# Two banks for the last half's roots, and v's second weights issued by ScalarE's queue

## The chip, the cores and the metric

The kernel runs on one core of one Trainium2 chip. The metric is the device time of one execution in microseconds. Before the change it is 700.87 us, the median of three runs (700.78 to 701.20).

A core has engines that run side by side, each through its own instructions in order: TensorE (PE in the profile, its loading of weights PEld), VectorE (DVE), ScalarE (ACT), GpSimd (POOL) and SyncE (SP), which only issues transfers. ScalarE and GpSimd can issue transfers as well; such an instruction stands in the engine's queue like any other, and what is behind it waits until it is issued.

## What is computed

One trunk layer on a sequence of 512 positions and 1024 channels, and a last RMS norm:

```python
h = rms_norm(x, norm_mix_g[l])
proj = h @ w_in[l]
cb, cc, cin, q, k, v, f_logit, g_logit = jnp.split(proj, split_idx, axis=-1)
u = causal_dwconv(cc * cin, conv_mix_w[l])
y_conv = (cb * u) @ w_out_conv[l]
o = forgetting_attention(q, k, v, log_f)      # heads of 64
y_attn = o @ w_out_attn[l]
x = x + (g_conv * y_conv + g_attn * y_attn) @ w_o[l]
h = rms_norm(x, norm_ffn_g[l])
up = causal_dwconv(h @ w_up[l], conv_ffn_w[l])
a, b = jnp.split(up, 2, axis=-1)
x = x + (jax.nn.silu(a) * b) @ w_down[l]
return rms_norm(x, norm_f_g)
```

`rms_norm` divides each position by the root of the mean of its squares (plus 1e-6) and scales each channel by a weight. Everything is float32.

## The kernel before

The activations lie transposed: 128 channels on the partitions, eight blocks of channels (kb = 0 to 7), 512 positions along the free dimension. Each float32 operand of a product is split into a high and a low part that TensorE can multiply in one pass each, and every product is three matmuls: high by high, weights' low by high, weights' high by low. For a weight tile, ScalarE (VectorE for the first two) makes the high part `wh`, VectorE the low part `wl`; for x, ScalarE makes `xgh` (line 468, with the norm's weight as a scale) and VectorE `xgl` (line 481).

**The start.** v comes first, since the rest of the attention needs it: eight blocks kb, each with weights `raw_v{kb}` (128 x 520) and a block of x, `xs{kb}` (128 x 512). TensorE works through them in order, 24 matmuls each, into six banks of PSUM: `pa0` to `pa3` (one per 128 positions) and `pb0`, `pb1`. Block kb = 0 is cut into halves of 256 positions: ScalarE converts the first half, then the second. In TensorE's order the four matmuls of the first half come first, then the four of the second half, each with the high parts, and so on. The transfers are issued in the order x0 (a first half of x with the norm's weights), v0 (its first 264 columns by ScalarE's queue, the rest by SyncE's), the second half of x's first block, then x1, v1, x2, v2 and so on, all by SyncE's queue (`load` and `load_x`). Before the first of these, seven matmuls on a tile of ones (`warm`, line 106) keep TensorE at work.

Eight semaphores (DMAHW0 to DMAHW7) are handed to the transfers of these queues in turn, in the order of the program. A transfer that gets a semaphore for the second time first waits until the earlier one on it has landed.

**The end.** The last blocks of channels (m = 6 and 7) of the down projection are summed in two halves of 256 positions, t = 0 and t = 1 (`plain7`). For each half `fin_sum` adds the residual, squares it (ScalarE, line 1210) and scales it; `fin_col` sums the squares over the channels by TensorE (`pc_n`, line 344) and takes the root (ScalarE) and its reciprocal (VectorE); `fin_out` spreads the reciprocal over all partitions by two matmuls into a bank of PSUM (`pb_n`, line 363), multiplies the eight blocks of channels by it, and issues their transfers out. VectorE multiplies blocks 0 to 5 in four products, reading the roots from PSUM (line 1226). [...]

## Time and profile before

| | us |
|---|---|
| median of three runs | 700.87 |
| the profiled execution | 700.85 |
| its span, first to last instruction | 699.1 |
| TensorE busy in the span | 688.4 |
| first matmul on v's weights, pa (start) | 4.08 |
| reciprocal of the second half (start) | 689.28 |
| GpSimd's last product (start, length) | 692.75, 1.26 |
| issue of the last transfer out (start) | 694.04 |

Times in the trace are counted from the span's start. A row of a timeline gives start, length, engine, line, operation, output and inputs, and in brackets how long the engine stood idle before and what ended it. "SPq" and "ACTq" are the issuing of transfers by SyncE and ScalarE. A row with x2 stands for two instructions in one piece. In a table by windows, each engine's busy time in the window is given with the number of its instructions, then the granted clock of TensorE, the share of the DMA engines' time that was busy, and the rate in GB/s.

### The profile page before, as it was taken

To read this page: it belongs to the slowest core of one execution; us is meant where nothing else is said; L and a number is where in the kernel's file an instruction comes from. 1 tells how busy PE (TensorE), PEld (TensorE's weight loads), DVE (VectorE), ACT (ScalarE), POOL (GpSimd) and SP (SyncE) were. 2 spreads that over 40 slices of the span, in tenths; PEclk is the share of its full clock that TensorE was granted. 3 is DMA by queue.
4 is the path that set the end of the run, shared out by engine and by line. 5 is a ranking of instruction groups with operands and counts; after the bars stand their busy time and mean duration, and the time that the engine had idled before them with its cause. 6 is when DMAs were issued, how large, how long until landed. Compare 5 with 4: busy or idle time off the path is not lost.

```text
span 699.1 us, 14571 instructions
## 1 busy us (share of the span) xinstructions
PE 688.4 (98%) x5978; PEld 686.1 (98%) x5978; DVE 506.6 (72%) x806; ACT 346.6 (50%) x551; POOL 159.6 (23%) x180
## 2 busy tenths in 40 slices
PE   9999999999999999999999999999999999999994
PEld 9999999999999999999999999999999999999994
DVE  6678777786687777764577877777775677877783
ACT  5574656555664443543445443455443345444662
POOL 5124646434011001035221212220000221200001
PEclk9999999999999999999999999999999999999998
DMA  8527877567359868758566647588675554334513
GB/s 313 184 85 204 206 153 186 132 167 177 96 143 272 254 179 241 233 183 206 144 156 175 168 111 214 144 182 224 192 225 178 147 147 99 102 99 139 161 60 121
DMA packets 54466, 118.91 MB, mean 170 GB/s; under 512 B 4960, under 2 KB 24416, under 8 KB 54400
## 3 DMA queue, kind: packets, MB, share of 16 engines
q1 hardware_dynamic: 39104, 96.55, 43.0%
q0 software_dynamic: 14576, 20.75, 18.6%
q8 instruction: 47, 0.77, 0.4%
q10 hardware_dynamic: 720, 0.69, 0.3%
q14 instruction: 19, 0.16, 0.1%
HBM read 115.80 MB, written 35.13 MB: 216 GB/s over the span
## 4 chain that ended last, share of the span: by engine, by line
PE 95%; DVE 2%; ACT 1%; issue 1%; ACTq 0%; POOLq 0%; POOL 0%; DVEq 0%
PE p_up L283 26%; PE p_in L283 14%; PE dn L301 13%; PE gs L301 8%; PE p_up L301 8%; PE p_wo L283 6%; PE yc L301 3%; PE ya L283 3%; PE pa L491 2%; PE pb L493 2%; PE p_g L283 2%; PE o L672 2%; PE tp L657 1%; PE pdA L283 1%; PE pdB L283 1%
## 5 line engine op out<-in xcount | busy, mean ns | idle before, releaser
L283 PE MATMUL p_up<-x1h,wh_up 128*128 128x256 f32 x536 | 104.8, 277 | 0.0
L283 PE MATMUL p_up<-x1l,wh_up 128*128 128x256 f32 x536 | 104.4, 276 | 0.0
L283 PE MATMUL p_up<-x1h,wl_up 128*128 128x256 f32 x536 | 104.3, 276 | 0.0
L250 ACT ACTIVATE wh_up<-raw_up 128x1024 fp32r<-128x1024 f32 x44 | 46.6, 1060 | 83.8 <-PE p_up L283 74.5
L139 POOL DMA_DIRECT2D sum<-in_wst_dram x51 | 52.7, 1108 | 125.3 <-DMA sum<-sum 89.1
L283 PEld LDWEIGHTS p_up<-x1h,wh_up 128*128 128x128 f32 x536 | 80.7, 188 | 0.5 <-issue 0.5
L283 PEld LDWEIGHTS p_up<-x1l,wh_up 128*128 128x128 f32 x536 | 80.8, 188 | 0.0
L283 PEld LDWEIGHTS p_up<-x1h,wl_up 128*128 128x128 f32 x536 | 80.6, 188 | 0.0
L254 DVE TENSOR_TENSOR wl_up<-raw_up,wh_up 128x1024 fp32r<-128x1024 f32 x44 | 54.1, 1230 | 16.1 <-ACT wh_up L250 16.1
L250 ACT ACTIVATE wh_F<-raw_F 128x1024 fp32r<-128x1024 f32 (+1 forms) x32 | 33.6, 1049 | 58.2 <-PE ya L283 25.9
L283 PE MATMUL p_in<-xgh,wh_in 128*128 128x256 f32 x288 | 56.8, 279 | 0.0
L283 PE MATMUL p_in<-xgh,wl_in 128*128 128x256 f32 x288 | 56.5, 277 | 0.1
L283 PE MATMUL p_in<-xgl,wh_in 128*128 128x256 f32 x288 | 56.4, 277 | 0.0
L989 DVE TENSOR_TENSOR fz<-p_up,rb_n 128x512 f32<-128x512 f32 x44 | 30.3, 690 | 32.4 <-PE p_up L283 32.4
L254 DVE TENSOR_TENSOR wl_F<-raw_F,wh_F 128x1024 fp32r<-128x1024 f32 (+1 forms) x32 | 38.6, 1207 | 20.0 <-ACT wh_F L250 19.3
L283 PEld LDWEIGHTS p_in<-xgh,wh_in 128*128 128x128 f32 x288 | 44.7, 188 | 0.7
L1002 POOL TENSOR_TENSOR ge<-fu,fu 128x512 f32<-128x512 f32 x11 | 17.1, 1552 | 120.2 <-DVE fu L586 107.2
L283 PEld LDWEIGHTS p_in<-xgh,wl_in 128*128 128x128 f32 x288 | 43.5, 188 | 0.3 <-DVE wl_in L254 0.3
L283 PEld LDWEIGHTS p_in<-xgl,wh_in 128*128 128x128 f32 x288 | 43.6, 188 | 0.0
L250 ACT ACTIVATE wh_P<-raw_P 128x768 fp32r<-128x768 f32 (+1 forms) x32 | 26.6, 832 | 27.3 <-PE dn L301 15.0
L301 PE MATMUL p_up<-x1h,wh_up 128*128 128x256 f32 x168 | 40.2, 276 | 0.0
L301 PE MATMUL p_up<-x1l,wh_up 128*128 128x256 f32 x168 | 40.2, 276 | 0.0
(319 smaller groups left out, 2033.1 us busy)
## 6 DMA issues: line engine op xcount, KB each, us to landing
raw_up<-in_wup_dram SPq DMA_DIRECT2D x44, 512.0 KB, 4.4
raw_F<-sum SPq DMA_DIRECT2D x31, 512.0 KB, 4.9
raw_in<-in_win_dram SPq DMA_DIRECT2D x24, 512.0 KB, 4.6
raw_P<-in_wst_dram SPq DMA_DIRECT2D x31, 384.0 KB, 3.6
sum<-in_wst_dram POOLq DMA_DIRECT2D x31, 256.0 KB, 5.7
sum<-in_wst_dram SPq DMA_DIRECT2D x15, 512.0 KB, 6.1
sum<-in_wst_dram POOLq DMA_DIRECT2D x15, 512.0 KB, 8.0
sum<-sum SPq DMA_DIRECT2D x30, 256.0 KB, 6.4
```

The costliest lines, as they stand in the source:

```text
L139: return lambda: keep(nc.gpsimd.dma_start(dst, src, accum_op=ALU.add))
L250: ins = nc.scalar.activation(hi, raw, AF.Copy)
L254: ins = nc.vector.tensor_sub(lo, raw, hi.bitcast(F32))
L283: keep(nc.tensor.matmul(out[:, cs], w, x[:, cs], start=start and i == 0 and c == 0, stop=stop and i == 2 and c == len(cut) - 1,))
L301: keep(nc.tensor.matmul(out, wl if x == 1 else wh, xl if x == 2 else xh, start=opens and bk not in seen, stop=closes and bk not in left,))
L491: keep(nc.tensor.matmul(pa[t][:, :VW], xt, w[:, :VW], start=start, stop=stop))
L493: keep(nc.tensor.matmul(pb[t], xt, w[:, VW:], start=start and t % 2 == 0, stop=stop and t % 2 == 1))
L657: keep(nc.tensor.transpose(tp[:, ks], pt[:, ks], ident))
L672: keep(nc.tensor.matmul(o[:, os_], vv[:, kb, pr, e, :], x[:, kb, cs], start=e == 0 and kb == 0 and i == 0, stop=e == 1 and kb == nk - 1 an ...
L989: nc.vector.tensor_mul(z, p, rb2)
L1002: keep(nc.gpsimd.tensor_mul(ge, a.rearrange(halves_of, h=2), b.rearrange(halves_of, h=2)))
```

## The change

There are two independent edits.

The first is at the start. `load` issues nothing for `raw_v1`; inside the conversion of x's block 0, ScalarE's queue issues that transfer, after the first half's conversion and before the second half's:

```diff
-            else:
+            elif k > 1:
                 keep(nc.sync.dma_start(raw[:, :ncol], src))
...
             for cs in cuts:
                 keep(nc.scalar.activation(xgh[:, kb, cs], x_of(kb, cs), AF.Copy, scale=g1(kb)))
+                if kb == 0 and cs.start == 0:
+                    keep(nc.scalar.dma_start(raws[1], stream[1][1]))
```

The second is in `fin_out`. In the first half (t = 0) the copy of the roots for GpSimd comes before VectorE's products instead of after them. In the second half the roots are made twice, in banks 4 and 2, one for VectorE and one for the copy. VectorE has three products of two blocks each instead of four, and the transfers out are four of two blocks each; in the second half ScalarE's queue issues the second and the last of them (GpSimd's).

```diff
-        pb = rstd_bc(rc, 2, (1, 4)[t], f"n3{t}")[:, : S // 2]
+        bks = ((1, 1), (4, 2))[t]
+        pb = rstd_bc(rc, 2, bks[0], f"n3{t}")[:, : S // 2]
+        pr = rstd_bc(rc, 2, bks[1], f"n3{t}r")[:, : S // 2] if t else pb
         rs = fp.tile([P, S], F32, tag="fu", name=f"rs{t}", bufs=3)[:, : S // 2]
-        parts_ = ((0, 1), (1, 3), (3, 5), (5, 6), (6, 8))
-        for a, b in parts_[:4]:
-            y = x1[:, a:b, hs]
-            keep(nc.vector.tensor_mul(y, y, pb.unsqueeze(1).to_broadcast([P, b - a, S // 2])))
-        keep(nc.scalar.activation(rs, pb, AF.Copy))
-        y = x1[:, 6:8, hs]
-        keep(nc.gpsimd.tensor_mul(y, y, rs.unsqueeze(1).to_broadcast([P, 2, S // 2])))
-        for g in (0, 1, 2, 3, 4):
-            a, b = parts_[g]
-            keep((nc.sync, nc.scalar)[t * (g in (1, 2))].dma_start(outT[:, a:b, hs], x1[:, a:b, hs]))
+
+        def by(e, r, g):
+            y = x1[:, 2 * g : 2 * g + 2, hs]
+            keep(e.tensor_mul(y, y, r.unsqueeze(1).to_broadcast([P, 2, S // 2])))
+
+        def copy():
+            keep(nc.scalar.activation(rs, pr, AF.Copy))
+
+        if t == 0:
+            copy()
+        for g in range(3):
+            by(nc.vector, pb, g)
+        if t:
+            copy()
+        by(nc.gpsimd, rs, 3)
+        for g in range(4):
+            keep((nc.sync, nc.scalar)[t * (g % 2)].dma_start(
+                outT[:, 2 * g : 2 * g + 2, hs], x1[:, 2 * g : 2 * g + 2, hs]
+            ))
```

How this moves instructions, at three places. First ScalarE at the start of the program, before (`xgh<-x` is the first half of block 0, `xgh<-xs,x` with 128x256 the second half, the one with 128x512 block kb = 1; in brackets the semaphores that each waits for):

```order
L204 DMA raw_v_132<-in_wv_dram 128x264
L468 ACTIVATE xgh<-x_130 128x256 [waits DMAHW0_49]
L468 ACTIVATE xgh<-xs_135,x_130 128x256 [waits DMAHW2_49]
L468 ACTIVATE xgh<-xs_135,x_130 128x512 [waits DMAHW3_49]
L455 ACTIVATE ssq_123<-x_130 128x256
```

and after:

```order
L204 DMA raw_v_132<-in_wv_dram 128x264
L468 ACTIVATE xgh<-x_130 128x256 [waits DMAHW0_49]
L470 DMA raw_v_138<-in_wv_dram 128x520 [waits DMAHW3_49]
L468 ACTIVATE xgh<-xs_135,x_130 128x256 [waits DMAHW2_49]
L468 ACTIVATE xgh<-xs_135,x_130 128x512
L455 ACTIVATE ssq_123<-x_130 128x256
```

The transfer stands ahead of the second half's conversion and waits for DMAHW3, the semaphore of x's block kb = 1; the conversion of that block needs no wait of its own any more.

TensorE's first matmuls on v, which are the same before and after but for their line numbers (here of the changed program; `pa_124` and `pa_125` take the first half of the positions, `pa_126` and `pa_127` the second):

```order
L493 MATMUL pa_124<-wh_v_151,xgh 128x264 [waits DVE_49,Activation_49]
L493 MATMUL pa_125<-wh_v_151,xgh 128x264
L495 MATMUL pb_128<-wh_v_151,xgh 128x256 [waits DVE_49]
L495 MATMUL pb_128<-wh_v_151,xgh 128x256
L493 MATMUL pa_126<-wh_v_151,xgh 128x264 [waits Activation_49]
L493 MATMUL pa_127<-wh_v_151,xgh 128x264
```

`pa_126` waits for ScalarE's second conversion, which now stands behind the transfer.

Then ScalarE at the end, before (`rs` is the copy of the roots, `sq_11` the square of the last block, `ms_n` the root):

```order
L350 ACTIVATE ms_n_8760<-pc_n_8755,ex 128x2 [waits PE_49]
L1227 ACTIVATE rs_8776<-pb_n_8773 128x256 [waits DVE_49,PE_49]
L1210 ACTIVATE sq_11_8800<-pdB_8636 128x256 [waits PE_49]
L1211 ACTIVATE x_4017<-pdB_8636,vec 128x256
L350 ACTIVATE ms_n_8812<-pc_n_8807,ex 128x2 [waits PE_49]
L1227 ACTIVATE rs_8825<-pb_n_8822 128x256 [waits DVE_49,PE_49]
L1232 DMA out_dram<-x_4017 128x2x256
L1232 DMA out_dram<-x_4017 128x2x256 [waits DMAHW6_49]
```

and after:

```order
L350 ACTIVATE ms_n_8760<-pc_n_8755,ex 128x2 [waits PE_49]
L1233 ACTIVATE rs_8776<-pb_n_8773 128x256 [waits PE_49]
L1212 ACTIVATE sq_11_8798<-pdB_8636 128x256 [waits DVE_49,PE_49]
L1213 ACTIVATE x_4017<-pdB_8636,vec 128x256
L350 ACTIVATE ms_n_8810<-pc_n_8805,ex 128x2 [waits PE_49]
L1233 ACTIVATE rs_8826<-pb_n31r 128x256 [waits PE_49]
L1243 DMA out_dram<-x_4017 128x2x256 [waits DVE_49]
L1243 DMA out_dram<-x_4017 128x2x256 [waits Pool_49]
```

Both copies wait for TensorE alone. The square's wait for VectorE is for the addition of the sums of squares before the reciprocal of the first half, not for the products. On VectorE the first half's products now wait for ScalarE's copy.

## The prediction

> **What bounds the kernel now.** I read the page first, then the chain of waits over the first 10 us, the timelines of the first and the last stretch, and the table by windows there.

> ```profile
> span 699.1 us, 14571 instructions
> ...
> PE 95%; DVE 2%; ACT 1%; issue 1%; ACTq 0%; POOLq 0%; POOL 0%; DVEq 0%
> ...
> PEld p_in L283 <- DVE wl_in L254: 0.3, 1, 0.3
> ```

> TensorE (PE) is 95% of the chain. The profiled execution took 700.85 us, 1.8 us more than its span and 0.02 us from the median, 700.87. So the sum can be made against 700.85. Nothing in the middle is edited: what counts is how early TensorE gets through its first blocks, and what is left after its last matmul. A delay at the start passes through whole, because between start and end the list of waits has nothing longer for TensorE than 0.3 us for a part of weights (its last row above; PEld is TensorE's loading of weights).

> The start, by the chain of waits (start, length, what):

> ```profile
> 1.05 3.35 PE warm L106 x14
> ...
> 5.39 0.56 PE pa L491 x2
> ...
> 6.82 0.42 PE pb L493 x2
> 7.25 0.25 PE pa L491 x2
> ...
> 8.45 0.23 PE pb L493 x2
> 8.68 0.30 PE pa L491
> ```

> From 1.05 on TensorE never stops. The first block of v (kb = 0) takes twelve pairs of matmuls, from 4.40 to 8.68. A pair takes about 0.43 until some 7.1, and 0.24 afterwards: the clock rises there, though the column of the granted clock reads 1.00 on both sides.

> ```profile
> 0.30:3.70 3.40, 2.65 (x12) 2.65 (x13) 0.23 (x2) 1.99 (x3) 2.92 (x13) 1.00 0.57 156
> 3.70:7.10 3.40, 3.40 (x17) 3.31 (x16) 2.30 (x5) 1.18 (x3) 3.22 (x7) 1.00 0.83 236
> ```

> In these windows (length, busy time of PE first) 2.65 us of work in 3.40 had not raised the clock; 3.40 of 3.40 had.

> **The start: what the change does.** ScalarE (ACT) and VectorE (DVE) there, by the timeline:

> ```profile
> 1.04 0.43 ACTq L204 DMA_DIRECT2D raw_v<-in_wv_dram  x1
> ...
> 3.64 0.91 DVE L248 CAST wh_v<-raw_v 128x264 fp32r<-128x264 f32 x2 [2.64 <-DMA raw_v<-in_wv_dram]
> ...
> 4.58 0.51 ACT L468 ACTIVATE xgh<-xs,x 128x256 fp32r<-128x256 f32 x1 [1.13 <-DMA xs<-in_xT_dram]
> ...
> 6.43 0.72 ACT L468 ACTIVATE xgh<-xs,x 128x512 fp32r<-128x512 f32 x1 [1.33 <-DMA xs<-in_xT_dram]
> ...
> 7.49 0.99 DVE L248 CAST wh_v<-raw_v 128x520 fp32r<-128x520 f32 x1 [1.42 <-DMA raw_v<-in_wv_dram]
> ```

> The transfer of v's second weights (raw_v1) goes from SyncE's queue to ScalarE's, between the two halves of the first conversion. The order shows that it waits there for DMAHW3, the semaphore on which the conversion of x's second block (kb = 1) waited before. So ScalarE stands until that block has landed. In the trace this is at 6.43. Queued behind are the second half of the first conversion (at 4.58 before) and all the rest of ScalarE. For that half waits TensorE's third pair (pa of positions 256 to 511), and TensorE works in order.

> Step by step: released at 6.43; the transfer's issue 0.43 (the row at 1.04), so 6.86; the half's conversion 0.51, so 7.37; some 0.05 to TensorE. It resumes at 7.42 where it went on at 5.39: a stall of 2.03 us with ten of the twelve pairs still to come. How long they take is set by the clock, which the trace does not show after a gap; I bound it:
> - Low: the clock is up at 7.1 as before. Ten pairs of 0.24 end at 9.82. But raw_v1 is then the last to come. The only such transfer by ScalarE's queue at the start went from 1.04 to 3.64, 2.6 us; from 6.43 this is 9.03, and with the 0.99 of the cast TensorE has its weights at 10.02, against 8.68 before. +1.3 us.
> - Middle: the clock needs another 3.4 us of unbroken work, as in 3.70:7.10, so until 10.8. By then 3.4 / 0.43 = 7.9 pairs are done, 2.1 follow at 0.24, end 11.3 against 8.68: +2.6 us. The cast at 10.02 is covered by TensorE's slow work.
> - High: it needs as long as the first time, 6.05 us from 1.05 to 7.1, so until 13.47. By then 14.1 pairs are done, which before stood at 8.68 + 4.1 x 0.24 = 9.66: +3.8 us.

> I take the middle, since the row nearest to it is the only full stretch that raised the clock; the first window, with 78% of work, did not, so a stretch with a stall of 2.03 us in it (3.70:7.10 would hold about half) should not either.

> [...]

> What the edit saves is nothing: SyncE's queue loses one issue of about half a microsecond, so x's third block and v's third weights come a little earlier, but TensorE needs those only one block of 2.9 us later than raw_v1. If raw_v1 came later than 11.3 instead of 9.03 it would cost its excess; 2.3 us cover that.

> **The end: what the change does.** Before (start, length; in brackets the idle time ahead and its releaser):

> ```profile
> 685.59 1.95 DVE L1226 TENSOR_TENSOR x<-x,pb_n 128x256 f32<-128x256 f32 x4 [1.16 <-PE pb_n L363]
> ...
> 686.68 0.28 PE L283 MATMUL pdB<-gl,wh_dp 128*128 128x256 f32 x1
> ...
> 687.64 0.38 ACT L1227 ACTIVATE rs<-pb_n 128x256 f32<-128x256 f32 x1 [3.40 <-DVE x L1226]
> ...
> 687.92 0.38 ACT L1210 ACTIVATE sq<-pdB 128x256 f32<-128x256 f32 x1
> ...
> 688.35 0.52 PEld L344 LDWEIGHTS pc_n<-ones,sq 128*128 128x128 f32 x4 [0.78 <-ACT sq L1210]
> ...
> 688.99 0.26 ACT L350 ACTIVATE ms_n<-pc_n,ex 128x2 f32<-128x2 f32 x1 [0.33 <-PE pc_n L344]
> ...
> 689.28 0.17 DVE L352 RECIPROCAL rc_n<-ms_n 128x2 f32<-128x2 f32 x1 [1.74 <-ACT ms_n L350]
> ...
> 689.61 0.61 PE L363 MATMUL pb_n<-ident,rc_n 128*128 128x128 f32 x4
> ...
> 690.25 1.95 DVE L1226 TENSOR_TENSOR x<-x,pb_n 128x256 f32<-128x256 f32 x4 [0.80 <-PE pb_n L363]
> ...
> 692.29 0.38 ACT L1227 ACTIVATE rs<-pb_n 128x256 f32<-128x256 f32 x1 [3.04 <-DVE x L1226]
> ...
> 692.75 1.26 POOL L1229 TENSOR_TENSOR x<-x,rs 128x512 f32<-128x512 f32 x1 [3.38 <-ACT rs L1227]
> ```

> *First half.* The copy of the roots (rs, 687.64) waited for VectorE's four products, and the square of the last product (687.92) queued behind it. Now the copy goes first (685.59), the products follow some 0.43 later and end at 687.9, and the square waits for nothing on VectorE that is late, only for TensorE's last matmul (686.68), through at about 687.0. TensorE's sum of squares then starts behind its own work ahead, which takes away the 0.78 idle. The reciprocal comes at 688.50, after the products with 0.6 to spare. -0.78 us for all that follows; between 0 and 0.78.

> *Second half.* Two more matmuls of the roots fill a second bank: four more entries, of which the row at 689.61 has four in 0.61, overlapping, so some 0.48 more. VectorE starts at 690.25 - 0.78 = 689.47. The second bank is full 0.45 to 0.5 later, at 689.95; copy 0.38, then 0.08, so GpSimd (POOL) starts at 690.45 beside VectorE and is through at 691.7, not at 694.01. The last transfer leaves when GpSimd is through; in the trace:

> ```profile
> 690.59 0.68 DVE L1226 TENSOR_TENSOR x<-x,pb_n 128x512 f32<-128x512 f32 x1
> ...
> 690.70 0.34 SPq L1232 DMA_DIRECT2D out_dram<-x  x1
> ...
> 694.04 0.38 SPq L1232 DMA_DIRECT2D out_dram<-x  x1
> ```

> So it goes at 691.75, 2.3 earlier. But four transfers of 256 KB must pass:

> ```profile
> 691.50:691.75 0.25, 0.00 (x0) 0.00 (x0) 0.25 (x1) 0.00 (x0) 0.00 (x0) 1.00 0.72 258
> 693.25:694.75 1.50, 0.00 (x0) 0.00 (x0) 0.00 (x0) 0.00 (x0) 0.77 (x1) 0.50 1.09 385
> ...
> 695.50:695.75 0.25, 0.00 (x0) 0.00 (x0) 0.00 (x0) 0.00 (x0) 0.00 (x0) 0.50 0.74 250
> 695.75:699.10 3.35, 0.00 (x0) 0.00 (x0) 0.00 (x0) 0.00 (x0) 0.00 (x0) 0.50 0.00 0
> ```

> (The last two columns are DMA share and GB/s.) Data flow 0.8 us after an issue (690.70 to 691.50), at 385 GB/s, so 262 KB take 0.69. VectorE's first two parts of eight are done at 689.47 + 0.68 = 690.15, data from 691.0; four transfers in a row end at 693.75, with small gaps 693.9, against 695.70. -1.8 us for the whole end. Bounds: -2.3 (the last issue alone) and -1.0 (nothing from the first half, since 0.78 falls away). What lies behind the last data, 3.35 us, stays.

> The nearest row with GpSimd working on as many elements while VectorE is busy is a product in the middle of the kernel:

> ```profile
> L1002 POOL TENSOR_TENSOR ge<-fu,fu 128x512 f32<-128x512 f32 x11 | 17.1, 1552 | 120.2 <-DVE fu L586 107.2
> ```

> It takes 1.55 there against 1.26 alone; 0.29 more would be half hidden by the transfers ahead. [...]

> **Sum.** 700.85 + 2.6 - 1.8 = 701.65; I say 701.6 us.

> **Rivals.**
> - *The clock stays low longer* (slower). The mechanism is the high bound, in TensorE after the stall: the clock takes as long to rise as at the start, and ten pairs and some of the next block go at half speed until 13.5. +3.8 - 1.8 = +2.0, 702.9. For it: 78% of work was not enough in 0.30:3.70. Against: after 7.42 there is no gap. [...] It decides above some 3.2 us at the start.
> - *The clock comes up on time*, or x's second block lands sooner with raw_v1 out of its queue: +1.3 - 1.8 = -0.5, 700.4. Against: half a window of work.
> - *No stall*: ScalarE is not held, and the change does what its words say, a transfer moved off a busy queue. Then the end alone counts, 699.0. The order speaks against it: the wait is on the instruction, ahead of the half that TensorE needs. It would take a landing before about 4.6, where the trace has 6.43.

> **How the numbers follow.** Forecast 0.60, late clock 0.20, early clock 0.14, no stall 0.06. Bounds together give -1.0 to +2.8; I leave out a little at each end: 700.2 to 703.2. A measurement here tells about 0.2%, 1.4 us, from no change. Faster by more needs no stall, 0.06. Slower by more: nearly all of the late clock and one part in eight of the forecast (a start of +2.9 with an end of -1.4), 0.27. Between: 0.67.

> **What would show it.** In the profile after: ScalarE's second half of xgh at about 6.9 instead of 4.58, TensorE idle some 2 us from 5.4, pairs of 0.43 after 7.4, the second block's matmuls at 11.3; at the end the square at 687.0 on before's scale, GpSimd beside VectorE, 3.35 us behind the last data. I am wrong if ScalarE's conversion stays at 4.6, if pairs of 0.24 follow the gap at once, or if the four last transfers leave gaps of 0.5.

## The result, and the profile after

The changed kernel takes 704.84 us (median of five runs, 702.78 to 706.49) against 700.94 for the kernel before (five runs beside them, 700.78 to 701.2): a ratio of 1.0055, with a 95% interval of 1.0037 to 1.0073. It is slower by about 3.9 us; the prediction was 701.6, in a range of 700.2 to 703.2. In these runs the changed kernel also scatters over 3.7 us where the one before stays within 0.4.

The profiled execution took 706.49 us, 1.77 more than its span, so it is read against before's 700.85. It is the slowest of the five, 1.65 above their median, so the losses read from it stand at the upper end. From the page:

```profile
span 704.7 us, 14570 instructions
...
PE 691.3 (98%) x5982; PEld 688.8 (98%) x5982; DVE 506.9 (72%) x804; ACT 346.6 (49%) x551; POOL 159.1 (23%) x180
...
PE 93%; DMA 2%; DVE 1%; ACT 1%; issue 1%; ACTq 0%; POOLq 0%; POOL 0%; SPq 0%; DVEq 0%
```

The chain of waits now contains DMA, 2% of it, which before's did not. Where, the chain over the first 20 us says (start, length, what):

```profile
2.12 5.75 DMA xs<-in_xT_dram
7.87 0.02 issue
7.89 6.74 DMA raw_v<-in_wv_dram
14.63 0.02 issue
14.65 0.44 DVE wh_v L248
15.10 0.14 issue
15.23 0.56 PE pa L493
...
18.17 0.22 PE pa L493
18.39 0.15 PE pb L495
18.54 0.12 PE pa L493
```

Two transfers in a row set the start. x's second block lands at 7.87; only then does ScalarE issue v's second weights, and they take 6.74 us. TensorE starts the second block of v at 15.23 where it started at 8.68 before, and at half the clock: matmuls of 0.22 until about 18.4, of 0.12 afterwards. Before's last matmul of the down projection stands at 686.68, here it is at 694.77 (below): the start costs 8.09 us in this execution.

TensorE's list of waits has the two stalls (total, times, longest):

```profile
PE pa L493 <- ACT xgh L468: 3.7, 1, 3.7
PE pa L493 <- DVE wh_v L248: 1.7, 1, 1.7
```

and the timeline who made them:

```profile
7.89 0.35 ACTq L470 DMA_DIRECT2D raw_v<-in_wv_dram  x1
...
8.29 1.12 ACT L468 ACTIVATE xgh<-xs,x 128x256 fp32r<-128x256 f32 x2 [4.84 <-DMA xs<-in_xT_dram]
...
8.85 0.81 PE L493 MATMUL pa<-wh_v,xgh 128*128 128x264 f32 x2 [3.73 <-ACT xgh L468]
...
14.65 0.43 DVE L248 CAST wh_v<-raw_v 128x520 fp32r<-128x520 f32 x1 [5.33 <-DMA raw_v<-in_wv_dram]
```

The first stall is ScalarE held in order at the transfer's wait, the second is the transfer itself. Of the 8.09 us, the two stalls are 5.4; the rest is half clock in the twelve pairs and beyond. The granted clock by windows (length, busy time of PE first; the column PEclk is the third from the right):

```profile
8.00:8.25 0.25, 0.00 (x0) 0.00 (x0) 0.00 (x0) 0.00 (x0) 0.25 (x2) 0.68 1.04 404
8.25:18.25 10.00, 7.72 (x34) 7.46 (x35) 4.05 (x7) 3.50 (x7) 1.66 (x3) 0.50 0.90 339
18.25:18.50 0.25, 0.25 (x4) 0.25 (x3) 0.11 (x1) 0.00 (x0) 0.00 (x0) 0.84 1.07 418
```

It fell at about 8.1, in the first stall, and was full again at 18.3.

The end, by the timeline of after (its scale is 8.09 us behind before's):

```profile
694.77 0.28 PE L283 MATMUL pdB<-gl,wh_dp 128*128 128x256 f32 x1
...
695.09 0.39 ACT L1212 ACTIVATE sq<-pdB 128x256 f32<-128x256 f32 x1 [1.02 <-PE pdB L283]
...
697.49 1.88 DVE L1230 TENSOR_TENSOR x<-x,pb_n 128x512 f32<-128x512 f32 x3 [0.80 <-PE pb_n L363]
697.93 0.38 ACT L1233 ACTIVATE rs<-pb_n31r 128x256 f32<-128x256 f32 x1 [1.45 <-PE pb_n31r L363]
698.40 1.27 POOL L1230 TENSOR_TENSOR x<-x,rs 128x512 f32<-128x512 f32 x1 [2.96 <-ACT rs L1233]
698.81 1.28 ACTq L1243 DMA_DIRECT2D out_dram<-x  x2
```

GpSimd multiplies blocks 6 and 7 by `rs`, the copy of the roots that ScalarE makes. The square no longer waits for VectorE's products of the first half, GpSimd works beside VectorE, and its product is as long there (1.27) as it was alone (1.26). The windows show the last data:

```profile
701.75:702.00 0.25, 0.00 (x0) 0.00 (x0) 0.00 (x0) 0.00 (x0) 0.00 (x0) 0.50 0.58 193
702.00:704.72 2.72, 0.00 (x0) 0.00 (x0) 0.00 (x0) 0.00 (x0) 0.00 (x0) 0.50 0.00 0
```

Data end about 7.2 us behind that last matmul (701.99 against 694.77), 9.1 before: 1.9 earlier. But behind the data only 2.73 us are left and no longer 3.3, so the end is shorter by 2.44: the span grew by 5.65, 8.09 less 2.44.

### The profile page after: what moved, and what is told of

The parts are those of the page before. It is cut to its first block, busy times and chain, and to the rows that moved or that the text cites. A ratio compares the mean times of both kernels' runs of the same rounds, so it can differ in the third digit from the quotient of the medians.

```text
span 704.7 us, 14570 instructions
## 1 busy us (share of the span) xinstructions
PE 691.3 (98%) x5982; PEld 688.8 (98%) x5982; DVE 506.9 (72%) x804; ACT 346.6 (49%) x551; POOL 159.1 (23%) x180
## 4 chain that ended last, share of the span: by engine, by line
PE 93%; DMA 2%; DVE 1%; ACT 1%; issue 1%; ACTq 0%; POOLq 0%; POOL 0%; SPq 0%; DVEq 0%
PE p_up L283 26%; PE p_in L283 14%; PE dn L301 13%; PE gs L301 8%; PE p_up L301 8%; PE p_wo L283 6%; PE yc L301 3%; PE ya L283 3%; PE pa L493 2%; PE p_g L283 2%; PE o L674 2%; PE pb L495 1%; PE tp L659 1%; PE pdA L283 1%; DMA raw_v<-in_wv_dram 1%
## 5 line engine op out<-in xcount | busy, mean ns | idle before, releaser
L283 PE MATMUL p_up<-x1h,wh_up 128*128 128x256 f32 x536 | 104.8, 277 | 0.0
L283 PE MATMUL p_up<-x1h,wl_up 128*128 128x256 f32 x536 | 104.4, 276 | 0.0
L283 PE MATMUL p_up<-x1l,wh_up 128*128 128x256 f32 x536 | 104.3, 276 | 0.0
L283 PEld LDWEIGHTS p_up<-x1h,wh_up 128*128 128x128 f32 x536 | 80.8, 188 | 0.5 <-issue 0.5
L283 PEld LDWEIGHTS p_up<-x1h,wl_up 128*128 128x128 f32 x536 | 80.7, 188 | 0.0
L283 PEld LDWEIGHTS p_up<-x1l,wh_up 128*128 128x128 f32 x536 | 80.6, 188 | 0.0
L254 DVE TENSOR_TENSOR wl_up<-raw_up,wh_up 128x1024 fp32r<-128x1024 f32 x44 | 54.1, 1230 | 16.8 <-ACT wh_up L250 16.8
L283 PE MATMUL p_in<-xgh,wh_in 128*128 128x256 f32 x288 | 56.8, 279 | 0.0
L283 PE MATMUL p_in<-xgh,wl_in 128*128 128x256 f32 x288 | 56.6, 278 | 0.1
L283 PE MATMUL p_in<-xgl,wh_in 128*128 128x256 f32 x288 | 56.5, 277 | 0.0
L254 DVE TENSOR_TENSOR wl_F<-raw_F,wh_F 128x1024 fp32r<-128x1024 f32 (+1 forms) x32 | 38.6, 1207 | 20.0 <-ACT wh_F L250 19.8
L283 PEld LDWEIGHTS p_in<-xgh,wh_in 128*128 128x128 f32 x288 | 44.7, 188 | 0.7
L1004 POOL TENSOR_TENSOR ge<-fu,fu 128x512 f32<-128x512 f32 x11 | 17.1, 1553 | 120.0 <-DVE fu L588 106.7
L283 PEld LDWEIGHTS p_in<-xgh,wl_in 128*128 128x128 f32 x288 | 43.6, 188 | 0.3 <-DVE wl_in L254 0.3
L283 PEld LDWEIGHTS p_in<-xgl,wh_in 128*128 128x128 f32 x288 | 43.6, 188 | 0.0
```

Of the source, the lines that this page charges most:

```text
L254: ins = nc.vector.tensor_sub(lo, raw, hi.bitcast(F32))
L283: keep(nc.tensor.matmul(out[:, cs], w, x[:, cs], start=start and i == 0 and c == 0, stop=stop and i == 2 and c == len(cut) - 1,))
L1004: keep(nc.gpsimd.tensor_mul(ge, a.rearrange(halves_of, h=2), b.rearrange(halves_of, h=2)))
```

## The experiments: the end

Two theories stood for the end. **D**: the data of the last transfers set it (the prediction). **G**: GpSimd sets it, with something that runs behind its last instruction. G came from the last pieces of the chain of waits, of before

```profile
689.38 3.34 issue
692.72 1.30 POOLq L1352
```

and of after:

```profile
694.14 1.29 POOL x L1230
695.43 2.93 issue
698.36 1.30 POOLq L1365
```

Both chains end in GpSimd's queue, neither in a transfer or in SyncE, which waits for the transfers. And in both the span ends 6.32 us behind the start of GpSimd's last product: 692.75 to 699.07, 698.40 to 704.72.

**e1_end_only**: the kernel before with the changed `fin_out` alone.

```diff
-        pb = rstd_bc(rc, 2, (1, 4)[t], f"n3{t}")[:, : S // 2]
+        bks = ((1, 1), (4, 2))[t]
+        pb = rstd_bc(rc, 2, bks[0], f"n3{t}")[:, : S // 2]
+        pr = rstd_bc(rc, 2, bks[1], f"n3{t}r")[:, : S // 2] if t else pb
...
+        if t == 0:
+            copy()
+        for g in range(3):
+            by(nc.vector, pb, g)
+        if t:
+            copy()
+        by(nc.gpsimd, rs, 3)
```

> The end as changed, the start as before. Theory G (the span ends 6.32 us after GpSimd's last product starts, as in the traces of before and of the change): that product starts 2.4 us earlier, so the time is 2.4 us lower, 698.5. Theory D (the span ends a fixed time after the last data, as the prediction had it): 1.8 to 1.9 lower, 699.0.

Measured: 698.5 us (698.35 to 700.12, seven runs) against 700.83, ratio 0.997 [0.9959, 0.998]. The end by itself is worth 2.3 us, as G says. Its chain of waits ends like the others, and 690.41 + 6.33 is its span, 696.74:

```profile
686.16 1.29 POOL x L1228
687.45 2.93 issue
690.38 1.30 POOLq L1363
```

**e11_first_half_only** and **e12_two_banks_only**: of the changed `fin_out`, one half of the positions each; the other half runs as before. Of e11 (e12 has `fin_old` for t = 0 in its place):

```diff
-    def fin_out(t, rc):
+    def fin_old(t, rc):
...
+    def fin_out(t, rc):
...
-    fin_out(1, rcB)
+    fin_old(1, rcB)
```

> The start as before; of the end only the first half as changed (the copy for GpSimd ahead of VectorE's products, three of them, four transfers), the second half as before. Theory G: the square no longer waits behind the copy, all of the second half comes 0.8 earlier, 700.1.

> The start as before; of the end only the second half as changed (two banks of roots, three products on VectorE beside GpSimd), the first half as before. Theory G: GpSimd's last product starts 0.9 behind VectorE's first and not 2.5, so 1.6 earlier, 699.3. Theory D (the transfers set the end): 1.1 lower at most, 699.8.

Measured: 700.01 us (ten runs, 699.95 to 700.26; 0.9987 [0.9978, 0.9996]) and 699.3 (ten runs, 699.18 to 699.35; 0.9975 [0.9966, 0.9984]), both beside a 700.94. That is -0.9 and -1.6, together -2.6; the two parts of `fin_out` add up to e1's -2.3 within the noise.

**e6_no_gpsimd_last**: e1, but in the last half VectorE makes the fourth product too. There is no copy, no second bank and no GpSimd behind the last matmul.

```diff
-        if t:
-            copy()
-        by(nc.gpsimd, rs, 3)
+        by(nc.vector if t else nc.gpsimd, pb if t else rs, 3)
```

> As e1, but in the last half VectorE makes the fourth product too, from the same bank, and GpSimd has nothing to do there. The last product ends 2.5 us after VectorE's start and not 2.2, so the last data come about as late as in e1 or 0.4 earlier. Theory G: GpSimd is through long before, the end is set by the transfers, 1.4 to 1.5 below e1, about 697. Theory D: 0 to 0.4 below e1.

Measured: 697.4 us (697.38 to 697.49, four runs), 0.9951 [0.9936, 0.9966]. Four products in a row on VectorE instead of three with GpSimd beside them, and the kernel is 1.1 us faster than e1. Its chain ends with VectorE's products:

```profile
689.44 0.69 DVE x L1229
690.13 0.60 DVEq L1362
690.73 1.20 DVE x L1229 x2
```

**e7_late_tiny_gpsimd**: e6, and one multiplication of a single column by GpSimd, which nothing reads, behind VectorE's last product.

```diff
+        if t:
+            fin_t = fp.tile([P, 1], F32, tag="fint", name="fin_t")
+            keep(nc.gpsimd.tensor_scalar(fin_t, x1[:, KB - 1, S - 1 : S], 1.0, 0.0, op0=ALU.mult, op1=ALU.add))
```

> As e6, with one product of a single column on GpSimd behind VectorE's last product, whose result nobody uses. No data goes out later. Theory G: the end moves to some 5 to 6.3 us behind this instruction, 1.9 to 3.1 above e6. Theory D: as e6 within 0.2.

Measured: 699.14 us (699.02 to 699.44, ten runs), 0.9976 [0.9966, 0.9986]: 1.74 more than e6, a little under what was expected. An instruction of 0.19 us that nobody waits for costs 1.7. The last data are at 693.9 in both kernels. Its row in the timeline:

```profile
692.09 0.19 POOL L1241 TENSOR_SCALAR fin_t<-x 128x1 f32<-128x1 f32 x1 [4.70 <-DVE x L1229]
```

What runs there stands in the raw trace, as an instruction DRAIN on GpSimd at the end of the program (us):

```
kernel   GpSimd's last work ends   its DRAIN          SyncE's waits end   span ends
before   694.02                    692.72 to 698.27   696.60              699.07
after    699.66                    698.36 to 703.93   702.88              704.72
e1       691.68                    690.38 to 695.94   694.89              696.74
e7       692.28                    692.05 to 696.54   694.83              697.3
e6       (none in the last half)   none so late       694.82              695.60
```

In the first four the DRAIN ends 4.3 us behind GpSimd's last instruction, 1.1 to 1.7 us later than all transfers are known to be through (SyncE's waits), and the span ends some 0.8 behind it. In e6 the end follows SyncE. So G holds: before and after the change GpSimd set the end, and the last data came second.

**e10_small_ends**: e6, with the last half's products and transfers cut into blocks of 1, 2, 2, 2 and 1, since now the data do count.

```diff
+        cuts = ((0, 1, 3, 5, 7, 8) if t else (0, 2, 4, 6, 8))
```

> As e6, with the last half's products cut into 1, 2, 2, 2 and 1 blocks and a transfer for each, so that data start to flow 0.24 earlier and the last transfer is half as long. In e6 nothing but the transfers is left to set the end (theory G), so 0.2 to 0.3 below e6, 697.15. If SyncE's and ScalarE's issuing is the limit there, it is as e6 or 0.1 above.

Measured: 697.25 us (697.1 to 697.31, four runs), 0.9947 [0.9934, 0.9961], 0.15 below e6, and 0.26 below it when each is taken against the kernel before that ran beside it. The two intervals overlap, so this last step is not clear of noise. It is the fastest median of all: the start as before, the first half as changed, no GpSimd in the last.

## The experiments: the start

Three things are in the edit: ScalarE is **held** until x's second block has landed; the transfer is issued **late**; and it stands in **another queue**. The theory after the result was that the late weights decide (L); the rivals were the hold, with its stall and its clock, and the queue.

**e2_head_only**: the first diff of the change alone, with the end as before.

> The start as changed, the end as before. Theory L (v's second weights, issued only after x's second block has landed, come in behind all that SyncE's queue had issued before): TensorE's second block of v starts at 14 to 15.5 us instead of 8.6, and the time is 4.3 to 8.1 us above before, by the clock, and scatters by some us. The prediction's theory (the stall between the two halves is the cost): 2.6 us above, 703.5.

Measured: 708.53 us (706.81 to 709.72, four runs), 1.0107 [1.0093, 1.0121]: +7.6. Its profile, of the slowest of the four (709.72), has ScalarE released at 8.19, the cast of v's second weights at 15.35, and stalls of TensorE of 3.3 and 2.6 us. +7.6 here and -2.3 in e1 make +5.3, where the median of the change is +3.9. That is inside the scatter of after (+1.8 to +5.6), so the two edits can be independent; closer than this the runs do not show it.

**e4_hold_only**: the transfer stays in SyncE's queue as before; ScalarE is held in the same place by converting x's second block there.

```diff
             for cs in cuts:
                 keep(nc.scalar.activation(xgh[:, kb, cs], x_of(kb, cs), AF.Copy, scale=g1(kb)))
+                if kb == 0 and cs.start == 0:
+                    keep(nc.scalar.activation(xgh[:, 1, :], x_of(1, slice(0, S)), AF.Copy, scale=g1(1)))
...
-        if kb == 1:
-            x_hi()
```

> As before, v's second weights by SyncE's queue in their old place; but ScalarE converts x's second block between the two halves of the first, so that it stands until that block has landed, as in the change. Only the hold is left. The prediction's theory: TensorE stalls from 5.4 to about 7.7 and the time is 2.6 to 3.8 us above before. Theory L: the hold is the smaller part of the change's cost, some 2.3 to 4 alone, and below e2 by 2 us or more.

Measured: 704.77 us (704.27 to 705.84, five runs), 1.0057 [1.0044, 1.0069]: +3.85. TensorE has one stall, and v's second weights are in time:

```profile
PE pa L491 <- ACT xgh L468: 2.9, 1, 2.9
```

The clock came up at 13.31. The hold with everything it does to the clock therefore costs about what the high bound of the prediction said (+3.8), and no more. That the two agree so well is partly luck: the stall was 2.9 us and not the 2.03 of the prediction.

**e5_late_no_hold**: the transfer is issued behind both halves of the first conversion, so that it holds nothing that the first block needs.

```diff
-                if kb == 0 and cs.start == 0:
+                if kb == 0 and cs.start > 0:
                     keep(nc.scalar.dma_start(raws[1], stream[1][1]))
```

> As e2, but the transfer stands behind both halves of the first conversion, ahead of the conversion of x's second block. ScalarE holds up nothing that TensorE needs early; only the weights are late. Theory L: TensorE runs on until 8.7, then idles until 14 to 15.5; time as e2 within 1 us. The prediction's theory: nothing is lost but what the weights come later than 8.6 by a price of 2.6 us from 6.4, that is 702.3 at most.

Measured: 709.53 us (707.1 to 710.32, four runs), 1.0127 [1.0111, 1.0142]: +8.6, no less than the whole edit at the start (e2, +7.6). There is no hold; its list of waits and its chain, of the fastest of the four, at 707.1:

```profile
PE pa L493 <- DVE wh_v L248: 4.9, 1, 4.9
```

```profile
2.11 5.30 DMA xs<-in_xT_dram
...
7.43 5.19 DMA raw_v<-in_wv_dram
...
12.65 0.44 DVE wh_v L248
```

So the late transfer is enough for the loss, and the hold is not needed for it. The two are no sum: with both, TensorE waits for the same late weights and the hold fills part of that time.

**e8_other_semaphore** was to give the transfer another semaphore to wait for, by a tiny transfer (one column, read by nobody) behind the loading loop.

```diff
+    shift = ap.tile([P, 1], F32, tag="shift", name="shift")
+    keep(nc.sync.dma_start(shift, vecs[:, :1]))
```

> As e2, with one tiny transfer (one column) on SyncE's queue ahead, so that the transfer of v's second weights gets another semaphore, that of v's first weights, which have landed by 3.6. Everything else of the start stands as in the change. Theory L in its full form (the wait for x's second block makes the issue late, the queue does the rest): issued at about 3.5, in about its old place, so the second block starts within 1 us of before; 700.9 to 701.9. If issuing by ScalarE's queue is itself the cost: 703 or more.

A miss: the tiny transfer came too late in the order, and the wait was the same as in e2. Measured 706.64 us (705.62 to 707.17, five runs), 1.0079 [1.0066, 1.0091]; issue at 7.48, cast at 12.53. It is in effect a second e2. In its execution (705.62, the fastest of the five) TensorE stalls for 3.1 us on ScalarE and not at all on the weights: its slow first block still covered them. So with the hold, the weights add to the loss only where they come later than that.

**e9_free_semaphore**: the same tiny transfer inside the loop, between the loads of x's second block and of v's second weights. The transfer by ScalarE now stands where the change puts it, but it waits for the transfer of v's first weights. That one landed at 3.46, when ScalarE's first conversion (to 3.44) was just through, so the wait holds nothing.

```diff
     for kb in range(1, AHEAD + 1):
         load_x(kb)
+        if kb == 1:
+            keep(nc.sync.dma_start(shift, vecs[:, :1]))
         load(kb)
```

> The start as changed, the end as before, and a tiny transfer (one column) on SyncE's queue between x's second and third block, so that the transfer of v's second weights, in the change's place between the two halves on ScalarE, now waits for the transfer of v's first weights instead of x's second block (e8 had put the tiny transfer too late, and its wait was still that of the change). Theory L (the wait for x's second block is the cause, by the hold and by the place in line that is lost): issued at about 3.6, landed by 8, TensorE's second block within 1 us of before, 700.9 to 701.9. If the place on ScalarE's queue is the cost: as e2 and e8, 705 or more.

Measured: 702.68 us (702.57 to 704.12, six runs), 1.0028 [1.0017, 1.004]: +1.75 where e2 has +7.6. Most of the loss hangs on which semaphore the transfer was given, that is on a wait for a transfer with which it has nothing to do. It did not go away altogether (700.9 to 701.9 was expected). The wait and the chain:

```profile
PE pa L496 <- DVE wh_v L248: 1.6, 1, 1.6
```

```profile
3.48 5.82 DMA raw_v<-in_wv_dram
...
9.32 0.44 DVE wh_v L248
```

The transfer left at 3.48, 0.9 us later than SyncE had issued it before (2.60), and still took 5.8 us; TensorE waits 1.6 us for it.

**e3_at_once**: the transfer directly behind that of v's first weights in ScalarE's queue, without any wait.

```diff
-                keep(nc.sync.dma_start(raw[:, :ncol], src))
+                keep((nc.sync, nc.scalar)[k == 1].dma_start(raw[:, :ncol], src))
```

> The end as before; v's second weights by ScalarE's queue, but issued directly behind the transfer of v's first weights, ahead of every conversion, with a semaphore that no earlier transfer has. If the wait ahead of the issue is what costs, this costs nothing: 700.9 within 0.6. If ScalarE's queue is slow for such a transfer once SyncE's queue is full, the second block of v starts some us late and the time is 703 or more.

Measured: 701.1 us (700.82 to 704.0, ten runs), 1.0007 [0.9998, 1.0017]: no difference. Issued at 1.51, when little is under way, the weights landed at 5.38, in 3.9 us. In this run ScalarE's queue by itself was no disadvantage, and it brought nothing either. In this execution TensorE waits for the second half of x's first block, converted at 5.58; with the start as before that stood between 4.14 and 5.42, so it is not shown that the early weights pushed it back.

```profile
PE pa L491 <- ACT xgh L468: 1.1, 1, 1.1
```

**e14_late_long_queue** and **e13_late_short_queue** (one execution each) ask why a late transfer is so slow. In e14 it is issued behind the conversion of x's second block, at 7.58. e13 is the same, but the program starts with two blocks loaded ahead and not four, so that fewer transfers were issued before; later blocks then come late as well, and only the transfer is compared, not the time.

```diff
-AHEAD = 4
+AHEAD = 2
```

> The start as in e5 (the end as before), but the transfer of v's second weights stands behind the conversion of x's second block and waits for no semaphore of its own: issued as late as in the change, at 6.5 to 7.5 us, with SyncE's queue as full as there. Whatever makes the transfer slow: 5 to 7 us from issue to cast, as in e5 (5.2) and the change (6.7).

> As e14, but only two blocks are loaded ahead and not four (three buffers for weights), so SyncE's queue holds fewer transfers when that of v's second weights is issued, at 6.5 to 7.5 us. If the transfers issued earlier are what it waits behind: 3 to 4.2 us from issue to cast, at least 1 us less than e14. If a transfer by ScalarE's queue takes long whatever is ahead: as e14 within 0.5. Its whole time says nothing, since the rest of the kernel loads less far ahead too.

Measured: 707.79 us and 710.81 us, beside 700.91. The transfer in the two chains, of e14:

```profile
7.58 5.75 DMA raw_v<-in_wv_dram
```

and of e13:

```profile
7.34 3.95 DMA raw_v<-in_wv_dram
```

With ten transfers issued ahead of it, as in e13, it takes 1.8 us less than with twelve, as in e14. In e14 its first data move at 10.44, 2.9 us after the issue, and in e13 at 8.79, after 1.45. One pair of executions is thin evidence, since the executions with twelve ahead differ among themselves by more than this (5.1 to 7.2 from issue to cast, below).

The traces hold a better one. A transfer of this size lands in sixteen shares, and the time of each is recorded. In all sixteen traces, the transfers that SyncE and ScalarE issued in the first 10 us begin to land in the order of their issue, whichever of the two issued them. Before, the first six were issued at 0.73, 1.04 (by ScalarE), 1.18, 1.65, 2.12 and 2.60 and began to land at 2.66, 3.15, 3.49, 3.86, 4.85 and 6.01. So a transfer has a place in one order of issue. In the changed kernel the weights are the 13th in it: what SyncE issued just before them, at 6.12, begins to land at 10.88, the weights at 11.54, what SyncE issued next at 13.49. Before, they were the 6th. In order of the place, with the issue, the end of the landing, VectorE's cast and the time from issue to cast (us):

```
kernel   place   issue   landed   cast    issue to cast
e3         4     1.51     5.38     6.53   5.0   (VectorE is late, not the weights)
before     6     2.60     7.47     7.49   4.9   SyncE's queue
e9         8     3.48     9.29     9.32   5.8   the tiny transfer ahead
e13       11     7.34    11.29    11.31   4.0   two blocks ahead
e8        13     7.48    12.50    12.53   5.1   the tiny transfer ahead
e5        13     7.43    12.63    12.65   5.2
e14       13     7.58    13.32    13.35   5.8
after     13     7.89    14.63    14.65   6.8
e2        13     8.19    15.32    15.35   7.2
```

The further back the place, the later the landing; and in the kernel before, the transfers in the 4th, 8th, 11th and 13th place landed at 4.56, 9.07, 11.09 and 12.43, all of SyncE's queue (the 4th only half a block of x). So the change moved the weights from the 6th place to the 13th, and in these traces their lateness goes with this loss of place. No run issues them late by SyncE's queue; that it would bring little is an estimate, from SyncE's transfer in the 13th place before, 5.6 us from issue to landing (6.79 to 12.43). Why the five executions with the 13th place lie 2.8 us apart is open.

## Why the prediction was wrong

**Right.** That ScalarE is held by the wait for x's second block, that TensorE's third pair stands behind it, that the clock is lost by this, and that a delay at the start goes through whole (7.99 us at TensorE's first sum of squares, 34.69 against 26.70, and 8.09 at the last matmul of the down projection). At the end: the reordering of the first half, -0.78 predicted and -0.9 measured alone (e11), with the square at 695.09, which is 687.0 on before's scale; the data, 1.8 us earlier predicted and 1.9 measured; GpSimd beside VectorE without a loss.

The last one was put into the sum without a row: no row of the kernel before shows that GpSimd beside VectorE takes no longer than its 1.26 us alone, and the nearest row, a product in the middle of the kernel, had 1.55. In the changed kernel the product took 1.27 us, 0.97 of them beside VectorE's products (697.49 to 699.37), which had one operand in PSUM (`pb_n`).

**The step that failed** is the price of the late transfer: "The only such transfer by ScalarE's queue at the start went from 1.04 to 3.64, 2.6 us; from 6.43 this is 9.03", and, resting on it, "The cast at 10.02 is covered by TensorE's slow work". The row at 1.04 was of an issue with one transfer ahead of it (SyncE's at 0.73), and of 264 columns where the second weights have 520. At 7.89 the transfer had twelve issued ahead of it and took 6.74 us. The cast came at 14.65, far beyond the 11.3 that the prediction named as the end of its cover. TensorE was through with its slow first block at 13.55, waited 1.7 us, and then went on at half clock to 18.3. A nearer row was there: the same weights by SyncE's queue, issued at 2.60 and cast at 7.49, 4.9 us with five transfers issued ahead. By it the cast would begin at 6.43 + 4.9 = 11.33 and the weights be there at 12.3, 1.0 beyond the cover of 11.3; the same sum would have said 702.7, slower. Nearer still is the place in the order of issue: the 13th transfer of the kernel before, issued at 6.79, landed at 12.43. With the cast that is 13.4, 2.1 beyond the cover, and the sum would have said 703.8.

**Mis-sized beside it.** x's second block released ScalarE at 7.89, not at 6.43. The value was that of one execution; in the fifteen other executions it lies between 6.44 and 8.19 (6.48 to 7.29 in the six whose start is that of before), and 6.43 is the earliest. It is not scatter alone. In the six kernels whose SyncE queue goes straight from x's second block to its third (after, e2, e5, e8, e13, e14) it lies between 7.33 and 8.19, in the ten others between 6.43 and 7.29. So taking the weights out of their place goes with a later landing of x's second block, the opposite of what the rival of the early clock allowed for; why is not shown. This alone is 1.5 us.

**The clock** did not go by the middle assumption (3.4 us of unbroken work from 7.42). With the weights in time, the hold alone cost +3.85 (e4) where this term had +2.6. The trace records from when to when the full clock was granted (us):

```
before  7.11 to 693.19
after   4.68 to 8.09, 18.33 to 701.00
e1      5.56 to 695.05
e2      5.91 to 9.33, 12.74 to 16.15, 19.57 to 702.23
e3      4.25 to 693.74
e4      13.31 to 695.98
e5      6.46 to 13.29, 16.70 to 699.37
```

**The end.** "What lies behind the last data, 3.35 us, stays" was wrong, and with a small effect. What lies there is no fixed tail behind the transfers but GpSimd's DRAIN, 4.3 us behind its last instruction. GpSimd's last product starts 2.44 us earlier against the last matmul (6.07 before, 3.63 after), and that is the gain, not the 1.9 of the data. The prediction had the lower bound of -2.3 for "the last issue alone" and put it aside for the data; that this number is near is luck, since it was reckoned for the last transfer and not for GpSimd. The chain of waits of before, read to its last row, already ended in POOLq.

**The sum.** 700.85 + 2.6 - 1.8 = 701.65 was predicted; 700.85 + 8.09 - 2.44 = 706.50 is the profiled execution, 706.49. The 4.85 us between them are 5.49 that the start cost more than predicted, less 0.64 that the end saved more. Of the 5.49, 1.70 is the first stall (3.73 for 2.03), 1.68 the second, and the remaining 2.1 the half clock beyond what was reckoned.

**What stays open.** How the loss at the start divides between hold, lateness and clock cannot be given as a sum, since they overlap: alone they cost +3.85 (e4) and +8.6 (e5), together +7.6 (e2). Why the changed kernel scatters from 702.8 to 706.5 was not followed run by run; the varying grid of the clock and the varying arrival of x's second block and of the weights could each do it. Nor was it tried whether another order of SyncE's early transfers would make e9 as fast as before.

## What to carry to other kernels

A transfer that is moved into an engine's own queue takes its semaphore's wait with it, and the engine can stand in order behind a transfer that has nothing to do with it (here ScalarE stood until 7.89 us; the start cost 7.6 us in e2 and 1.75 in e9, where the transfer waited for one that had landed). Look in the order at what it waits for, and price the transfer from a row of the same size at the same place in the order of issue, not from one of the first issues of the program (here 264 columns took 2.6 us in the 2nd place, and 520 columns 6.74 in the 13th). Read the chain of waits to its last row before saying what sets the end: where it ended in GpSimd's queue here, the data did not set the end (in e6 and e7 the last data are at 693.9 alike, and e7 takes 1.74 us more), and the cheapest gain was to keep GpSimd out of the last stretch (1.1 us, with more work for VectorE). A time read from one execution's first microseconds is a sample (x's second block released ScalarE between 6.43 and 8.19), so give it a range, and ask whether the change itself moves it.

## What the hardware showed that was not expected

- GpSimd's closing DRAIN ended 4.3 us after its last instruction in before, after, e1 and e7, whether that took 1.27 us or 0.19 us, and the span ended some 0.8 us behind it. One multiplication of a single column, which nobody waits for, cost 1.74 us (e7 against e6).
- Transfers issued by SyncE and by ScalarE began to land in the order of their issue in all sixteen traces. Weights in the 4th place of this order had landed at 5.38 us (e3), in the 6th at 7.47 (before), in the 13th at 12.50 to 15.32.
- After a window (3.41 us) with TensorE at work for 55% of it, the full clock was still granted (e5, 6.46 to 9.87); after 43% (e13, 9.93 to 13.34) and 13% (after, 4.68 to 8.09) it was not. Where it was not full, it did not rise after 60% and 78% (after, 11.50 to 14.91 and 8.09 to 11.50) and did after 91% (after, 14.91 to 18.33) and 94% (e3, 0.84 to 4.25). So 55% kept the full clock in one window, and 78% did not bring it back in another.
- How early the clock rose did not matter in three kernels whose start is that of before. It came at 7.11 before, at 5.56 in e1 and at 5.23 in e7, and the second block of v began at 8.62, 8.61 and 8.60: VectorE's cast of its weights ended at 8.45 to 8.48 in all three (starts by the timeline).
